# Gate weights of the first block issued from ScalarE, and two output transfers of the last set merged, in a ReGLU MLP

## The chip, the cores and the metric

The kernel runs on one core of a Trainium2 chip. The metric is the device time of one execution, in microseconds (us), as the median of several runs. Engines are named TensorE (PE), VectorE (DVE), ScalarE (ACT), GpSimd (POOL) and SyncE (SP); SP does no arithmetic here and issues most of the transfers. "SPq" in a row of the profile is SP's instruction queue, and a DMA row there is the issue of a transfer, not the transfer.

## The reference

```python
# x: 16 x 256 x 512, w1: 512 x 4096, w2: 2048 x 512, all float32
h = x @ w1
gate, value = np.split(h, 2, axis=-1)
h = np.maximum(gate, 0) * value
return (h @ w2).astype(np.float32)
```

## The kernel before

The 4096 rows of x are taken in four sets of 1024 (`NS` = 4), each of two halves of 512 (`TH`). The hidden size of 2048 is taken in 16 blocks of 128 (`NJ`). Both products are done in fp16 with Strassen's scheme (in Winograd's form): seven products P1 to P7 in place of eight, on sums of x blocks (`x_A..`, `x_S..`) and of weight blocks (`w_B..`, `w_T..`). A `Block` computes one hidden block of the first product with its gate and value; a `Pair` computes 128 rows of each half of the second product. `psx`, `psy` and `psw` are the PSUM banks X, Y and W in the rows of the profile. The first two blocks (`NPLAIN`) of set 0 are computed plainly, class `Plain`, because the sums of x are not ready yet.

PE's and DVE's instructions stay in the order in which they are written, and so do those of ACT, POOL and SP. So every engine runs a list written by hand, and a wait at its head holds all that stands behind it.

The start of the program is what the first part of the change touches. SP issues, in this order: blocks 0 and 1 of x (128 rows, 256 KB each, `fetch_first(0, (0, 1))`, L504); the weights of hidden block 0, first the gate columns and then the value columns (256 KB each, `load_w1`, L224, into the staging tile `w_stage`); blocks 2 and 3 of x; the weights of hidden block 1; four more blocks of x for the second half; and further weights. Blocks 2 and 3 of x, and those of the second half, land in tiles that are used as x tiles or row tiles later (`x_A`, `x_S`, `xh`), and that is how the rows name them: "x_S<-in_x_dram" at 3.23 us is block 3.

PE meanwhile does 28 small and one large matmul on constants (L155, L156) so that it is busy from the start. Then follow, in this order: transposes of x blocks 0 and 1 (L514; copied out of PSUM by DVE and ACT, L517); three filler matmuls (`keep_busy`, L161); the gate part of hidden block 0 for the first 256 columns (L328), which needs the gate weights copied to fp16 by POOL and DVE (`plain_w`, L479); four fillers; the value part; two fillers; the transposes of x block 2 (cast on DVE, L507); three fillers; the transposes of x block 3 (cast on POOL, L507); and the rest of the two plain blocks, with the transposes of the second half between them.

```python
    fetch_first(0, (0, 1))
    first_w = [load_w1(nc.sync, *wl[0])]
    fetch_first(0, (2, 3))
    first_w.append(load_w1(nc.sync, *wl[1]))
```

At the other end, a `Pair` leaves its four pieces of output in a tile `o` of 128 x 2 x 512 and sends them from SP (`send`, L377). Its products end in the order P2, P3 (the two column halves of the first half's rows) and P7, P4 (those of the second half's rows). Where `self.end` holds, each piece of 128 KB is sent as soon as it is written; otherwise the two pieces of one half go together as 256 KB. Before, `self.end` holds for pairs 0, 1 and 3 of the last set. The order of the last set is `LAST_ORDER`; its last product is P4 of pair 3.

Of the kernel before, what the change touches and what calls it, by code (L numbers as in the profile page):

```python
# [26 lines left out]
@with_exitstack  # L27
def kernel(ctx: ExitStack, tc: tile.TileContext, x, w1, w2, out):

    nc = tc.nc
    x2 = x.flatten_outer_dims()
    out2 = out.flatten_outer_dims()
    flagpool = ctx.enter_context(tc.tile_pool(name="flagpool", bufs=1))
    flag = flagpool.tile([1, 1], dt.int32, name="flag")
    with ExitStack() as fast:  # L40
        unfit = fast_way(fast, tc, x2, w1, w2, out2, flag)
    with tc.If(unfit > 0, label="general"):
        with ExitStack() as general:
            general_way(general, tc, x2, w1, w2, out2)
# [52 lines left out]
def fast_way(ctx, tc, x2, w1, w2, out2, flag):  # L97
# [9 lines left out]
    nc = tc.nc  # L107
# [3 lines left out]
    NS = T // (2 * TH)  # L111
    NJ = H // P
    NB = 2 * TH // P
# [107 lines left out]
    def load_w1(eng, jb, n, u, vs=(0, 1)):  # L221
        t = w_stage[:, u:u + n].rearrange("p u v -> p (u v)").rearrange("p (g e j) -> p g e j", g=2, e=4)
        for v in vs:
            eng.dma_start(out=t[:, v], in_=w1_v[v, :, :, jb * P:(jb + n) * P])  # L224
        return t.rearrange("p g (k b) j -> p k b g j", k=2)
# [18 lines left out]
    class Block:  # L244
        def __init__(self, xo, g, jb, in_halves=()):
            self.xo, self.g, self.jb, self.behind, self.in_halves = xo, g, jb, (), in_halves
# [99 lines left out]
    class Pair:  # L346
        def __init__(self, s, g, t):
            self.s, self.t, self.o = s, t, None
            self.end = s == NS - 1 and t != NB // 2 - 2
            o = {f"A{h + 1}{u + 1}": g[:, u * NJ // 2:(u + 1) * NJ // 2, h * TH + t * P:h * TH + (t + 1) * P]  # L350
                 for h in range(2) for u in range(2)}
            o.update({f"S{n + 1}": s_place[:, t % 2, n] for n in range(4)})
            self.op = o
# [93 lines left out]
    wl = [(jb, 1, jb) for jb in range(4)] + [(jb, 2, jb % 6) for jb in range(4, NJ, 2)]  # L447
# [54 lines left out]
    def fetch_first(h, bs):  # L502
        for b in bs:
            nc.sync.dma_start(out=xn[h][b], in_=x_nat[0, h, b])  # L504
# [22 lines left out]
        return psy.tile([P, TH], F32, name="Y", tag="Y")  # L527

    dve, act, pool = nc.vector.tensor_copy, nc.scalar.copy, nc.gpsimd.tensor_copy
    fetch_first(0, (0, 1))  # L530
    first_w = [load_w1(nc.sync, *wl[0])]
    fetch_first(0, (2, 3))
    first_w.append(load_w1(nc.sync, *wl[1]))
    make_identity(nc, ident)
# [284 lines left out]
```

## Time and profile before

| | |
|---|---|
| median of 3 runs | 307.82 us (307.44 to 308.31) |
| profiled execution, its own time | 308.68 us |
| its span, first to last instruction | 306.8 us |
| PE busy | 301.4 us, 98% |
| DVE busy | 237.9 us, 78% |
| ACT busy | 176.6 us, 58% |
| POOL busy | 149.9 us, 49% |
| mean granted TensorE clock | 0.999 |
| moved by DMA | 32.88 MB, mean 107 GB/s |

The profile is of one execution. A line such as "PE X L328 <- POOL w_B L479" means that the instruction of line 328 on PE that writes X waited for POOL's instruction of line 479 that writes `w_B`. The chain that ended last is followed back from the last instruction to what released each step, and in the timeline rows of one form that follow each other are merged, with the start, the length, the engine, the line, the operation and the count.

### The profile page before, as it was taken

The page shows a single profiled execution, that of the slowest core. Times are in us where ns is not written, and L with a number is a line of the kernel's source. Part 1 is how long each engine was busy: PE and PEld are TensorE (multiplying, and loading weights), DVE is VectorE, ACT ScalarE, POOL GpSimd, SP SyncE. Part 2 cuts the span into 40 slices and gives each one's busy share as a digit, 9 for nine tenths or more (in the row PEclk, how much of TensorE's full clock was granted, in tenths as well). Part 3 has the DMA queues.
Part 4 walks back from the last instruction along what each step waited for, and adds up shares of the span by engine and source line. Part 5 has one row for each costly group of instructions (what it writes and reads, how often), then busy time and mean ns, then how long its engine had stood idle before and what let it go on. Part 6 is the DMA issues. An engine that isn't in the chain of part 4 may idle for free.

```text
span 306.8 us, 5361 instructions
## 1 busy us (share of the span) xinstructions
PE 301.4 (98%) x1938; PEld 187.6 (61%) x1938; DVE 237.9 (78%) x393; ACT 176.6 (58%) x351; POOL 149.9 (49%) x187
## 2 busy tenths in 40 slices
PE   7999999999999999999999999999999999999995
PEld 6755554588844444478864444458885444447884
DVE  2599888899778888887627889888545888888861
ACT  2398886445865555537855555545866555553231
POOL 1549999800068999400019989900005899800100
PEclk9999999999999999999999999999999999999999
DMA  7996679955774242000355730000326110000133
GB/s 209 332 297 212 194 172 178 233 113 87 240 208 104 69 77 63 0 2 34 139 170 124 174 81 2 2 0 0 118 89 207 34 35 2 2 0 19 52 105 106
DMA packets 36894, 32.88 MB, mean 107 GB/s; under 512 B 14465, under 2 KB 32385, under 8 KB 36737
## 3 DMA queue, kind: packets, MB, share of 16 engines
q1 hardware_dynamic: 34592, 26.22, 28.5%
q0 software_dynamic: 2272, 6.29, 11.4%
q8 instruction: 16, 0.26, 0.4%
q14 instruction: 14, 0.11, 0.1%
HBM read 27.26 MB, written 12.58 MB: 130 GB/s over the span
## 4 chain that ended last, share of the span: by engine, by line
PE 96%; DMA 2%; SPq 1%; POOL 0%; issue 0%; DVE 0%; ACT 0%
PE Y L252 26%; PE X L252 17%; PE W L252 17%; PE Y L365 14%; PE X L365 9%; PE W L365 9%; DMA x_S<-in_x_dram 2%; PE X L328 1%; PE W L328 1%; PE Y L328 1%; PE Y L514 1%; SPq L504 0%; SPq L224 0%; POOL fold L507 0%; DVE warm L417 0%
## 5 line engine op out<-in xcount | busy, mean ns | idle before, releaser
L252 PEld LDWEIGHTS <-w_T 128*128 128x128 f16 x524 | 51.2, 98 | 54.3 <-POOL w_T L234 0.4
L186 POOL TENSOR_TENSOR fold<-xh 128x1024 f32<-128x1024 f16 x16 | 30.3, 1896 | 95.7 <-DMA xh<-x 68.4
L252 PE MATMUL X<-x_A,w_B 128*128 128x512 f16 x248 | 73.7, 379 | 0.0
L252 PE MATMUL Y<-x_S,w_T 128*128 128x512 f16 x220 | 65.4, 379 | 0.0
L252 PEld LDWEIGHTS <-w_B 128*128 128x128 f16 x372 | 36.3, 98 | 42.2 <-issue 0.2
L280 DVE SCALAR_TENSOR_TENSOR cc<-W,pu 128x512 f32<-128x512 f32 x62 | 42.9, 692 | 19.5 <-ACT pu L274 19.4
L260 ACT COPY Y<-X 128x512 f32<-128x512 f32 x62 | 35.4, 572 | 38.3 <-PE X L252 38.1
L274 ACT ACTIVATE pu<-Y 128x512 f32<-128x512 f32 x62 | 37.1, 598 | 33.8 <-PE Y L252 32.7
L189 POOL TENSOR_TENSOR fold<-fold 128x512 f32<-128x512 f32 (+2 forms) x96 | 51.8, 540 | 7.5
L365 PEld LDWEIGHTS <-w_stage 128*128 128x128 f16 x512 | 50.1, 98 | 5.8
L290 DVE SCALAR_TENSOR_TENSOR cc<-Y,pu 128x512 f32<-128x512 f32 x62 | 42.9, 692 | 6.5
L285 DVE SCALAR_TENSOR_TENSOR g<-X,cc 128x512 f16<-128x512 f32 x62 | 42.9, 691 | 2.3
L302 DVE SCALAR_TENSOR_TENSOR g<-Y,cc 128x512 f16<-128x512 f32 x62 | 42.3, 682 | 1.8 <-PE Y L252 1.8
L365 PEld LDWEIGHTS <-g 128*128 128x128 f16 x384 | 37.6, 98 | 8.2
L267 ACT ACTIVATE pu<-W 128x512 f32<-128x512 f32 x62 | 37.2, 600 | 0.4 <-PE W L252 0.2
L252 PE MATMUL W<-x_S,w_T 128*128 128x512 f16 (+1 forms) x152 | 36.9, 340 | 0.0
L252 PE MATMUL W<-x_S,w_B 128*128 128x512 f16 x124 | 36.9, 379 | 0.0
L252 PE MATMUL Y<-x_A,w_T 128*128 128x512 f16 x124 | 36.9, 379 | 0.0
L365 PE MATMUL X<-w,g 128*128 128x256 f16 x256 | 31.9, 273 | 0.0
L402 DVE SCALAR_TENSOR_TENSOR o<-W,pu 128x256 f32<-128x256 f32 x16 | 6.8, 423 | 21.8 <-PE W L365 21.8
L176 DVE TENSOR_TENSOR w_stage<-g 128x1024 f16<-128x1024 f16 x32 | 21.4, 686 | 0.2
L234 POOL TENSOR_TENSOR w_T<-w_stage,w_T 128x512 f16<-128x512 f32 (+1 forms) x14 | 15.4, 1098 | 5.7 <-DVE w_T L234 5.2
(100 smaller groups left out, 312.0 us busy)
## 6 DMA issues: line engine op xcount, KB each, us to landing
out_dram<-o SPq DMA_DIRECT2D x26, 256.0 KB, 2.0
w_stage<-in_w_dram SPq DMA_DIRECT2D x12, 512.0 KB, 5.3
x<-in_x_dram POOLq DMA_DIRECT2D x4, 1024.0 KB, 10.0
xh<-x SPq DMA_DIRECT2D x16, 256.0 KB, 3.3
w_stage<-in_w_dram SPq DMA_DIRECT2D x8, 256.0 KB, 6.2
w<-in_w_dram POOLq DMA_DIRECT2D x2, 1024.0 KB, 10.4
out_dram<-o SPq DMA_DIRECT2D x12, 128.0 KB, 1.7
x_S<-in_x_dram SPq DMA_DIRECT2D x4, 256.0 KB, 6.0
```

The source lines that it names most:

```text
L176: eng.tensor_tensor(o[n], o[i0], o[i1], op=op)
L186: nc.gpsimd.tensor_tensor(fold, t, t, op=MULT)
L189: nc.gpsimd.tensor_tensor(fold[:, :, :m], fold[:, :, :m], fold[:, :, m:2 * m], op=ADD)
L252: nc.tensor.matmul(ps[:, slice(*c)], wop[wn][:, b, self.jb * P:(self.jb + 1) * P], self.xo[xn][:, b, slice(*c)], start=fresh and b == c[0] ...
L260: nc.scalar.copy(out=self.Y, in_=self.X)
L267: nc.scalar.activation(self.p5, self.W, COPY, scale=GS)
L274: nc.scalar.activation(self.u2, self.Y, COPY, scale=GS)
L280: nc.vector.scalar_tensor_tensor(out=self.c12, in0=self.W, scalar=GS, in1=self.u2, op0=MULT, op1=ADD)
L285: nc.vector.scalar_tensor_tensor(out=self.g[:, self.jb, :TH], in0=self.X, scalar=0.0, in1=self.c12, op0=MAX, op1=MULT)
L290: nc.vector.scalar_tensor_tensor(out=self.c22, in0=self.Y, scalar=GS, in1=self.p5, op0=MULT, op1=ADD)
L302: nc.vector.scalar_tensor_tensor(out=self.g[:, self.jb, TH:], in0=self.Y, scalar=0.0, in1=self.c22, op0=MAX, op1=MULT)
L365: nc.tensor.matmul(ps, self.op[an][:, i], vop[wn][:, i], start=name in ("P1", "P5") and i == 0, stop=i == NJ // 2 - 1, skip_group_check=True)
```

## The change

ScalarE issues the transfer of the gate columns of hidden block 0, written ahead of the first two x transfers, and SP issues only the value columns of that block, in the old place behind the two x transfers. `load_w1` has always had the argument for the engine and for the parts to load. In the last set pair 1 no longer counts as an end pair: its four sends of 128 KB become two of 256 KB. Pair 2 was sent that way before; pairs 0 and 3 are still sent piece by piece.

```diff
@@ class Pair
-            self.end = s == NS - 1 and t != NB // 2 - 2
+            self.end = s == NS - 1 and t in (0, 3)
@@ fast_way
+    first_w = [load_w1(nc.scalar, *wl[0], (0,))]
     fetch_first(0, (0, 1))
-    first_w = [load_w1(nc.sync, *wl[0])]
+    load_w1(nc.sync, *wl[0], (1,))
     fetch_first(0, (2, 3))
     first_w.append(load_w1(nc.sync, *wl[1]))
```

## The prediction

> **What bounds the kernel now.** I read the page first, the waits of PE second, the chain that ended last third, and then the first 14 us piece by piece, because the edit sits at the two ends. The page: TensorE works nearly everywhere, and the DMA engines are fullest at the start.
>
> ```profile
> PE   7999999999999999999999999999999999999995
> DMA  7996679955774242000355730000326110000133
> ```
>
> Each digit is a slice of 7.67 us. Only the first and the last PE digit are below 9, so only time taken out of those two ends can shorten the run. The waits of TensorE's matmuls (us in total, times, longest) name the whole idle time:
>
> ```profile
> PE X L328 <- POOL w_B L479: 1.3, 1, 1.3
> PE Y L418 <- DVE warm L417: 0.9, 1, 0.9
> PE Y L155 <- PEq L803: 0.8, 1, 0.8
> ```
>
> The 1.3 us is the first gate matmul, waiting for the fp16 copy of the weights whose load is moved. It looks like the whole prize. The chain that ended last (start us, us, what) says otherwise:
>
> ```profile
> 2.13 0.51 SPq L224
> ...
> 2.68 0.51 SPq L504
> ...
> 3.23 6.06 DMA x_S<-in_x_dram
> 9.29 0.05 issue
> 9.34 0.63 POOL fold L507
> 9.96 0.05 issue
> 10.01 0.40 PE Y L514 x4
> ```
>
> It runs through block 3 of x (I call it x3): issued at 3.23, landed 9.29, cast on POOL, transposed at 10.01; from there PE is dense. The gate wait at 7.71 is not on it. How near it is comes from the timeline (start us, us, engine line op):
>
> ```profile
> 6.08 0.37 ACT L517 CAST x_A<-X 128x256 f16<-128x256 f32 x1 [0.48 <-PE X L514]
> 7.10 0.29 DVE L479 CAST w_B<-w_stage 128x256 f16<-128x256 f32 x1 [1.02 <-DMA w_stage<-in_w_dram]
> 7.71 0.61 PE L328 MATMUL X<-x_A,w_B 128*128 128x256 f16 x4 [1.33 <-POOL w_B L479]
> 9.47 0.49 PE L161 MATMUL Y<-warm 128*128 128x256 f16 x3
> 10.01 0.40 PE L514 MATMUL Y<-ident,fold 128*128 128x128 f16 x4
> ```
>
> PE is in order. From the gate matmul at 7.71 to the end of the last three filler matmuls (they start at 9.47, and at 0.11 us each, the step of the L161 rows, end at 9.80) it has 2.09 us of its own work, idle parts aside. x3's transposes could start at 9.80 and start at 10.01. So there are **two near-equal limits, 0.21 us apart**: the gate's copy, and x3. An earlier gate alone is worth nothing.
>
> What does x3 wait for? The stretches (us, PE busy, clock, DMA share, GB/s) of TensorE:
>
> ```profile
> 0.00:6.50 6.50, 5.60 (x40) 1.00 0.66 185
> 6.50:7.70 1.20, 0.00 (x0) 1.00 1.01 340
> 7.70:10.00 2.30, 2.25 (x21) 1.00 1.12 346
> 10.00:12.00 2.00, 1.99 (x24) 1.00 1.06 377
> 12.00:14.00 2.00, 2.00 (x23) 1.00 1.18 307
> ```
>
> From 6.5 us on the DMA engines are full (share 1.0 and more), and they are nearly full from 2 us (the one-microsecond stretches give 1.00, 0.94, 0.95, 0.81, 0.87 for 2 to 7). x3 spends 6.06 us in a queue, not in its issue. One more thing from the trace's completion records, sixteen for each transfer, one for each DMA engine: the gate's come at 4.45 to 5.16 us on fifteen engines and at 7.08 on the last. That late engine then also ends value (7.87), x2 (8.56) and x3 (9.29; the other fifteen had it by 8.55).
>
> **The change, part by part.** The sum is made against the profiled execution, 308.68 us (span 306.8 and 1.88 around it). The median of the runs shown is 307.82, so this execution is 0.86 slow; I carry differences over to the median.
>
> SP loses one issue: 0.43 us plus the 0.04 before the next. Value, x2, x3, both parts of block 1's weights and what follows are issued 0.47 us earlier. From the ninth transfer SP is held anyway (x_S issues: median 0.43 us, longest 1.84), so behind that point nothing is gained by a shorter list. SP computes nothing; only loads are queued there.
>
> ScalarE gains one issue, about 0.45 us by SP's rows. Its table load (1.28 us at 0.73) stands beside it; together they end near 2.5, and ScalarE's first copy starts at 5.23. Cost zero, cover 2.7 us. Should the table load come first, the gate is issued at 2.01 instead of 1.66, still ahead of ScalarE's work, and only SP's 0.47 is left. POOL issues no load here; its casts only wait for landings.
>
> The gate's landing: at the soonest 3.3 (0.74 plus the 2.6 that x0 takes alone in an empty queue), at the latest 7.08 as now, if the late engine is as late. I take 5.2, where fifteen engines already had it, since x0, x1 and gate must all pass by then. P1 of the first block then waits for x_A (ready at 6.45 today) and not for weights, and may start 1.0 us earlier (worked out below). PE then idles in front of value or of x2 or x3 instead.
>
> x3's landing is the term that counts. [...] Row first: x3 issued at 3.23, engines full, 6.06 us to land. [...] by the row it is less, since an earlier place in a full queue does not move the bytes ahead of it: x0, x1, gate, value and x2 still have to go first, the same 1.3 MB. What two queues can change is the ramp: between 1.7 and 2.6 us the tenth-microsecond slices average 202 GB/s, against some 390 just after, so 0.9 x (1 - 202/390) = 0.43 us of engine time is lost; two issuers starting together may fill half, 0.2 us. I take -0.2[...], and keep 0 and -0.47.
>
> Behind x3 come the rows of the second half: PE's transposes at 12.18 wait 0.45 for a cast of a block landed at about 11.7, in the same full queue. They move by the same 0.2 or PE waits there; there are only about 0.1 to 0.3 us of slack at each. After 14 us PE's matmuls wait for no input until the last one, and its weight loads only twice, 0.2 us each, for POOL's w_T; so a shift of this size lasts to the end.
>
> The merge: in the last set pair 1 sends twice 256 KB in place of four times 128 KB. SP loses two issues of 0.33 us. The tail (start, us):
>
> ```profile
> 302.44 0.89 PE Y L365 x8
> 303.35 0.39 ACT o L414
> 303.76 0.44 DVE warm L417
> ```
>
> Pair 1's last piece of o is written at 294.13 (ScalarE row at 293.74, 0.39 long), and an output of 256 KB takes 2.0 us to land against 1.7: done near 296.5, 7 us before the last piece. Its buffer is not needed again: pair 3 takes the slots of the first two pu2 tiles. So zero. The cover is those 7 us; uncovered it would cost 0.3. ScalarE's queue is a third one in use; no row prices its setting up, and I take zero, bounded by a few tenths either way inside the 1.88 around the span.
>
> Sum: -0.2 (x3 and its followers) + 0 (ScalarE) + 0 (merge) = 308.5 for the profiled execution, 307.6 for the median.
>
> **Rivals.** *The gate was what held the late engine.* If its 2 us of delay belongs to the position of that load, and vanishes, x3 lands with the fifteen others or sooner (at least 0.74 earlier) and the limit becomes x_A. x1 shares the engines with 256 KB more, about 0.87 us at 300 GB/s: it lands at 4.94 instead of 4.07; from the start of its transposes to the ready x_A are 1.67 us (4.78 to 6.45); P1 at about 6.7, 1.0 us earlier. Time 306.8. For it: fifteen engines are early. Against: nothing says why the one is late, and x2, x3 and the second half must all follow.
>
> *x1 falls behind the gate (slower).* [...] No row of before shows two such queues at once here; by the rows' one queue x1 lands at 4.07[...]. If the late engine is late again, x1 lands with it, at 7.08: x_A at 7.08 + 0.05 + 1.67 = 8.80, P1 at 8.85, x3's transposes at 8.85 + 2.09 = 10.94 in place of 10.01, that is +0.93, 308.75. It decides once x1 lands after 6.15 (10.01 - 2.09 - 0.1 - 1.67). For it: x1 has the longer way to PE than the gate, and the gate is put ahead of it. Against: it needs a stall of 2 us on one engine in just that load.
>
> *The change does nothing at all*: table load first, the same full queue: 307.8.
>
> **Numbers.** Chances: forecast 0.54, late engine gone 0.25, x1 late 0.13, nothing 0.08. A measurement of this kernel can tell about 0.3%, 0.92 us, from no change. The forecast and the last case lie within it. The gain of 1.0 is just beyond it, and a larger ramp gain or a saving in what lies around the span may add to it: faster 0.26. x1 late by the full amount is just beyond on the other side: slower 0.12. Same 0.62. Range 306.7 to 308.6: the -1.0 case to most of the +0.93 case; the likeliest case's own is 307.3 to 308.0.
>
> **What the changed profile would show.** The gate's cast on DVE directly behind the copies of x_A, and no 1.3 us of PE X L328 waiting for POOL w_B; a wait of the same size in front of value, x2 or x3; x3's cast on POOL at 9.1 instead of 9.34. ScalarE's issue at 0.74, the table load behind it. x1's transposes at 4.78 or a few tenths later. Tail unchanged from 303 us less the shift. I am wrong if x3's cast starts before 8.7 (gain near 1 us), or if L514's X transposes start after 6.2 (loss), or if the time outside the span moves.

## The result, and the profile after

The changed kernel takes 307.03 us (median of 6 runs, 306.84 to 307.43) against 307.95 us before (6 runs). The ratio is 0.9972, 95% interval 0.9959 to 0.9984: about 0.9 us shorter, within the stated range and just inside the 0.3% that was called no change. The forecast step was -0.2 us; the measured one is closer to the -1.0 of the first rival. The profiled execution takes 307.43 us, with a span of 305.6.

In what follows x0 to x3 are the first four blocks of x, and gate and value are the two weight loads of hidden block 0; SP or ScalarE issues each of them. The page's slices, to set beside those of before:

```profile
PE   8999999999999999999999999999999999999996
DMA  7996679955774260000355820000326110000133
```

Only the two end digits of PE rise. The waits of TensorE's matmuls (us in total, times, longest):

```profile
PE Y L418 <- DVE warm L417: 0.9, 1, 0.9
PE Y L155 <- PEq L804: 0.8, 1, 0.8
PE X L514 <- DMA x_A<-in_x_dram: 0.6, 1, 0.6
PE Y L514 <- POOL fold L507: 0.2, 1, 0.2
```

The 1.3 us behind the gate's copy is gone. In its place are a wait for x1 (0.6 us) and one for x3 (0.2 us). The beginning in order of time (start us, us, engine line op):

```profile
0.74 0.44 ACTq L224 DMA_DIRECT2D w_stage<-in_w_dram  x1
1.21 1.28 ACT L517 ACT_TABLE_LOAD   x1 [1.21 <-PEq L804]
4.75 0.39 POOL L479 CAST w_B<-w_stage 128x256 f16<-128x256 f32 x1 [3.45 <-DMA w_stage<-in_w_dram]
5.45 0.66 PE L514 MATMUL X<-ident,x_A 128*128 128x128 f32 x4 [0.64 <-DMA x_A<-in_x_dram]
6.41 0.83 PE L328 MATMUL X<-x_A,w_B 128*128 128x256 f16 x4
9.19 0.40 PE L514 MATMUL Y<-ident,fold 128*128 128x128 f16 x4 [0.23 <-POOL fold L507]
```

ScalarE issues at 0.74 with the table load behind it, at no cost: the load ends at 2.49, and ScalarE's first copy starts at 4.85. The gate has landed by 4.70; x1 comes only at 5.41 (4.07 before), and TensorE waits 0.64 us for it, with the three fillers on constants held behind. The first gate matmul starts 1.3 us earlier than before. The chain that ended last (start us, us, what) still leads to x3:

```profile
2.13 0.51 SPq L504
...
2.68 5.79 DMA x_S<-in_x_dram
8.46 0.05 issue
8.52 0.63 POOL fold L507
9.14 0.05 issue
9.19 0.40 PE Y L514 x4
```

x3 lands at 8.46 where it landed at 9.29, and its transposes start at 9.19 where they started at 10.01. From there everything moves as one piece: from the start of these transposes to the last copy of o on ScalarE are 293.34 us before and 293.38 after. The stretches of the start (us, PE busy, clock, DMA share, GB/s):

```profile
0.00:6.50 6.50, 5.08 (x41) 1.00 0.72 210
6.50:7.70 1.20, 1.14 (x10) 1.00 1.08 346
7.70:10.00 2.30, 2.07 (x27) 1.00 1.12 345
10.00:12.00 2.00, 2.00 (x19) 1.00 1.08 368
```

TensorE now works from 6.5 to 7.7; the DMA engines moved 210 GB/s up to 6.5 us in place of 185. The difference lies between 4 and 7 us. First before, where PE is followed by the other engines, then after; the last two numbers are again DMA share and GB/s:

```profile
4.00:5.00 1.00, 1.00 (x6) 0.86 (x5) 0.19 (x1) 0.00 (x0) 0.00 (x0) 1.00 0.95 256
5.00:6.00 1.00, 1.00 (x7) 0.92 (x7) 0.57 (x2) 0.37 (x1) 0.00 (x0) 1.00 0.81 201
6.00:7.00 1.00, 0.38 (x4) 0.09 (x1) 0.09 (x1) 0.37 (x1) 0.00 (x0) 1.00 0.87 259
```

```profile
4.00:5.00 1.00, 0.81 (x5) 1.00 0.96 317
5.00:6.00 1.00, 0.55 (x5) 1.00 0.96 301
6.00:7.00 1.00, 0.94 (x9) 1.00 1.00 355
```

The engines are a little busier and move about a third more. The end is not only shifted (start us, us, what):

```profile
301.66 0.89 PE Y L365 x8
...
302.57 0.39 ACT o L414
...
302.99 0.44 DVE warm L417
```

This copy of o starts 0.78 us earlier, but the span is 1.14 us shorter. The other 0.36 us lies behind the last landing, at 305.44 before and 304.68 after. SP closes the program with waits on counters (semaphores); the trace lists sixteen raises of a counter for each send, for the last one at 305.30 to 305.44 us before and at 304.54 to 304.68 after. The instructions of that line on SP, first from 305.44 us on in the kernel before, then from 304.68 on in the kernel after:

```profile
L814 SPq EVENT_SEMAPHORE  x7: 28/28/28, 305.5 to 305.8; - x7
```

```profile
L815 SPq EVENT_SEMAPHORE  x1: 28/28/28, 304.7 to 304.7; - x1
```

Seven waits of 0.06 us each (start to start) stand against one. That accounts for 6 x 0.06 = 0.36 us.

### The profile page after: what moved, and what is told of

Same layout as the page of the kernel before. It is cut to its first block, busy times and chain, and to the rows that moved or that the text cites. A ratio compares the mean times of both kernels' runs of the same rounds, so it can differ in the third digit from the quotient of the medians.

```text
span 305.6 us, 5356 instructions
## 1 busy us (share of the span) xinstructions
PE 301.0 (98%) x1938; PEld 186.8 (61%) x1938; DVE 238.0 (78%) x393; ACT 176.5 (58%) x351; POOL 149.6 (49%) x187
## 4 chain that ended last, share of the span: by engine, by line
PE 96%; DMA 2%; SPq 1%; POOL 0%; issue 0%; DVE 0%; ACT 0%
PE Y L252 26%; PE X L252 18%; PE W L252 18%; PE Y L365 14%; PE X L365 9%; PE W L365 9%; DMA x_S<-in_x_dram 2%; PE X L328 1%; PE W L328 1%; PE Y L328 1%; PE Y L514 1%; SPq L504 0%; POOL fold L507 0%; DVE warm L417 0%; SPq L224 0%
```

## The experiments

**The kernel before, once more.**

> The kernel before, unchanged, to see whether the late DMA engine belongs to it or to one execution. If the gate load behind x0 and x1 on one queue is what makes an engine late, the gate's copies on POOL and DVE again start near 7.1 us and block 3's cast on POOL near 9.3; ratio 1.000. If lateness is a matter of chance, the cast of block 3 starts anywhere from 8.4 to 9.4, and the ratio is still 1.000.

Measured: 1.0003 (0.9994 to 1.0011); x3 landed at 8.56, not at 9.29, and no DMA engine was 2 us late with the gate (5.26). So the very late DMA engine on which I built two rivals belongs to single executions. The kernel still took 308.06 us in the median: the time before is not explained by that engine.

**Each part alone.** Only the start of the diff:

```diff
+    first_w = [load_w1(nc.scalar, *wl[0], (0,))]
     fetch_first(0, (0, 1))
-    first_w = [load_w1(nc.sync, *wl[0])]
+    load_w1(nc.sync, *wl[0], (1,))
```

> Only the gate load moved to ScalarE, the sends left in four pieces. My theory: all of the gain is here: ratio 0.997, block 3's cast near 8.5 us, a wait of about 0.6 us for x1. Rival (the merge brings a part, or the end does): a ratio of 0.999 or more and the rest in the merge alone.

Measured: 0.9975 (0.9964 to 0.9986). x3 landed at 7.55. And only the merge:

```diff
-            self.end = s == NS - 1 and t != NB // 2 - 2
+            self.end = s == NS - 1 and t in (0, 3)
```

> Only the two sends merged. My theory: 1.000 within 0.001, chain of the end unchanged, since these pieces land 7 us before the last. Rival: two issues of 0.33 us less on SP show as 0.3 to 0.6 us, ratio 0.998 to 0.999.

Measured: 0.9983 (0.9974 to 0.9991), 0.5 us less. My theory that the merge costs and brings nothing fell. The profile shows why: one closing wait stands behind the last landing, as in the changed kernel. In the trace of before the sends take eight counters in turn, numbers 102 to 109, and SP's closing waits go over them in this order. With fourteen sends after the last row load, the last send falls on the second counter of that round, 103. Its wait stands at 305.46 us, and those on the other six, whose sends had landed by 303.71, still stand behind it, at 305.52 to 305.82. With two sends fewer it falls on the last of the eight (109 in the changed kernel, its wait at 304.70).

**The same number of sends, with pair 1 merged and pair 2 in pieces.** It asks whether merging pair 1 is worth something by itself, with the number of sends and the place of the last one in the round as before.

```diff
-            self.end = s == NS - 1 and t != NB // 2 - 2
+            self.end = s == NS - 1 and t in (0, 2, 3)
```

> The start of before; pair 1 of the last set sends merged as in the change, but pair 2 sends in pieces, so SP issues as many sends as before. My new theory, the drain: SP's closing waits go over the completion counters in a fixed order, transfers take the counters in turn, and what counts is how many waits stand behind the counter of the last send (seven in before, one with the merge alone, 0.06 us each). Then this kernel has seven again, ratio 1.000. Rival: larger and fewer sends of pair 1 are worth 0.4 us by themselves, ratio 0.9985.

Measured: 1.0003 (0.9996 to 1.0009). From 304.80 us on, where its last send landed, SP's closing line reads:

```profile
L814 SPq EVENT_SEMAPHORE  x7: 28/28/28, 304.8 to 305.2; - x7
```

Pair 1 is merged as in the change, and nothing is gained. This run can't part fewer sends as such from the place of the last one, since both are as before. The place rests on the tails: from the last landing to the end of the span are 1.32 to 1.34 us in all ten profiles with fourteen sends, and 0.96 in all four with twelve. Of the 0.5 us (0.3 to 0.8) measured for the merge alone the waits explain 0.36; whether there is more is not shown.

**Do the parts add?** The changed kernel and the gate-only kernel were run again, with more runs.

> The changed kernel beside the others on one chip. If the two parts add up (0.9975 and 0.9983), ratio 0.9958; if the first comparison was right, 0.997 and a part of one is lost in the other. Block 3's cast on POOL between 7.6 and 8.5 us; one wait of the drain behind the last landing.

> The gate-only kernel again, to see whether the two parts add. If they add: 0.9985 or so here (0.36 us over the whole change at 0.9973), seven waits behind the last landing. If the merge is lost behind the moved gate, 0.9973 and as long a tail as with the change.

Measured: 0.9974 (0.9965 to 0.9984) for the change, 0.9981 (0.9974 to 0.9988; 16 runs) for the gate alone, whose profile has seven waits behind the last landing. With the first value of the gate alone the product of the parts, 0.9958, lay outside the interval of the change. With the longer measurement it is 0.9981 x 0.9983 = 0.9964, whose difference to 0.9974 is inside the intervals. So the parts may well add: about 0.6 us from the gate and 0.36 us, the count of closing waits, from the merge. In the second run of the change the chain no longer goes through x3 (start us, us, what):

```profile
1.20 4.18 DMA x_A<-in_x_dram
...
5.43 0.66 PE X L514 x4
6.09 0.33 PE Y L161 x3
6.42 0.57 PE X L328 x4
6.99 0.44 PE Y L161 x4
7.42 0.44 PE W L328 x4
7.86 0.22 PE Y L161 x2
8.08 0.22 PE Y L514 x4
8.30 0.33 PE Y L161 x3
```

It comes from x1 over the gate matmuls and TensorE's own list, fillers included, to x3's transposes at 8.68. Both gate-only profiles have the same chain (8.55 and 8.72).

**The order without the second queue.** First the gate ahead of both x blocks, all on SP:

```diff
+    first_w = [load_w1(nc.sync, *wl[0], (0,))]
     fetch_first(0, (0, 1))
-    first_w = [load_w1(nc.sync, *wl[0])]
+    load_w1(nc.sync, *wl[0], (1,))
```

> The gate goes ahead of x0 and x1, but on SP's own queue, value in its old place: the order changes, the queue does not. If the order (gate ahead of the x blocks) brings the gain: gate landed by about 3.5 us, x1 by 5.0, block 3's cast near 8.5, ratio 0.997 or a little less. If a second queue is needed: block 3 lands near 9.3 as before, since SP's list is as long as before, and the ratio is 1.000; then nothing is won by order. If x1 is held back by more than 1 us: over 1.000.

Measured: 1.0054 (1.0038 to 1.007), slower by 1.7 us. x1 landed at 6.23, only 0.8 us later than with the change, and x3 at 8.93. What is different stands in the lengths of the rows (start us, us, engine line op):

```profile
6.27 1.12 PE L514 MATMUL X<-ident,x_A 128*128 128x128 f32 x4 [0.84 <-DMA x_A<-in_x_dram]
7.18 0.85 PE L161 MATMUL Y<-warm 128*128 128x256 f16 x3
7.82 1.06 PE L328 MATMUL X<-x_A,w_B 128*128 128x256 f16 x4
```

The same four transposes take 0.66 us after the change, the same fillers 0.49 in the second run of it: here TensorE still runs at about half speed. The trace's clock record puts full speed at 9.71 us here; in the other profiles it is between 3.76 and 6.79. My reading was that the rise of the clock was put off while TensorE waited for x1. The profile is one of five runs of 309.65 to 309.89 us. Three others took 308.1 to 308.7, and four took 310.2 to 310.4 with a mean granted clock of 0.994 in place of 0.998; the profile does not speak for those. To test the reading, six fillers go, on top of the gate's move, between the transposes of x0 and those of x1:

```diff
     turn_first(xo, 0, 0, halves(*YS), (dve, act))
+    keep_busy(6)
     XS = [new_x(), new_x()]
     turn_first(xo, 0, 1, halves(*XS), (dve, act))
```

> The gate ahead of x0 and x1 on SP (1.0054 before), now with six filler matmuls between the transposes of x0 and those of x1, where TensorE was idle. If the loss came from the idle time, which put off the rise of the clock (full speed from 9.7 us in that profile), the clock is up by 7 us and the ratio falls to 0.998 to 1.000. If the loss came from x1's late landing itself, it stays at 1.005.

Measured: 1.0013 (1.0003 to 1.0024). The profiled run, of 309.25 us, is one of the longest of its 22. In it one DMA engine was 2.1 us late with x1, which landed at 7.59, later than ever, and yet:

```profile
7.63 0.66 PE L514 MATMUL X<-ident,x_A 128*128 128x128 f32 x4 [1.30 <-DMA x_A<-in_x_dram]
8.13 0.49 PE L161 MATMUL Y<-warm 128*128 128x256 f16 x3
```

That is full speed (from 5.7 us), and no run of the 22 has a granted clock below 0.998. The fillers win back 0.4% of the 0.54%: most of the loss was the clock. The remaining 0.13% may be x1's lateness; this profile shows that it costs, but not that it makes up the median. Second, the gate between x0 and x1:

```diff
-    fetch_first(0, (0, 1))
-    first_w = [load_w1(nc.sync, *wl[0])]
+    fetch_first(0, (0,))
+    first_w = [load_w1(nc.sync, *wl[0], (0,))]
+    fetch_first(0, (1,))
+    load_w1(nc.sync, *wl[0], (1,))
```

> All on SP, in the order x0, gate, x1, value: the loads mix as they do with two queues, and SP's list is as long as before. If what counts is that gate and value no longer follow each other in one queue, block 3's cast starts at 8.0 or earlier and the ratio is about 0.9975. If the second queue (or the shorter list of SP) is needed, 1.000. If x1 comes so late that PE idles before its clock has risen, as in the run with the gate first, over 1.002, with the x1 transposes at half speed.

Measured: 1.0071 (1.0047 to 1.0095). Its seven runs fall in two groups, 307.68 and 307.87 us, and 310.09 to 311.10. The profile is of the first group: full speed from 3.9 us, x1 landed at 6.01, x3 at 8.22, and the clock stayed up over a wait of 1.42 us for x1. There is no profile of the second group, but each run's granted clock is on record: 0.993 or 0.994 in four of its five runs, 1.000 and 0.999 in the first group. In the one profile here with 0.993 (the kernel before without fillers, below) the clock rose early and then fell to half for 3.41 us, so a fall, and not a late rise, is the likelier reading for those four. The fifth has 0.998, as the profile with the gate first.

**Another load on ScalarE's queue.** x1 in place of the gate:

```diff
-    fetch_first(0, (0, 1))
+    nc.scalar.dma_start(out=xn[0][1], in_=x_nat[0, 0, 1])
+    fetch_first(0, (0,))
     first_w = [load_w1(nc.sync, *wl[0])]
```

> x1 instead of the gate is issued on ScalarE; sends as before. SP's list is shorter by one as in the gate-only kernel, x1 is not behind the gate, and gate and value follow each other again on SP. If the shorter list or the second queue is the cause, ratio 0.9975 or a little less, and no wait for x1 at its transposes. If moving the gate away from value is the cause, 1.000 and block 3's cast at 8.5 to 9.3.

Measured: 0.9983 (0.9975 to 0.9991), the same as the gate alone in its longer measurement. x1 landed at 4.17 and x0 at 4.38, before the gate (5.10), and x3 at 8.45. That profile is of a run of 307.99 us, the second longest of thirteen, and its x3 comes about as late as in the repeat of before (8.56); so the gain is shown by the times, not by the profile. So it does not matter much which of the first three loads leaves SP's list; that gate and value follow each other again on SP does not undo the gain.

**Without the fillers.** The nine behind the first gate matmuls are left out, once after and once before the change:

```diff
     plain[0].part("gate", *first_half, cols(0, 2))
-    keep_busy(4)
     plain[0].part("value", *first_half, cols(0, 2))
...
-    keep_busy(2)
     turn_first(xo, 0, 2, [t[:, 2] for t in turned], (dve, act))
-    keep_busy(3)
     turn_first(xo, 0, 3, [t[:, 3] for t in turned], (dve, act))
```

> The changed kernel without the nine filler matmuls that stand behind the first gate matmuls (four, two and three). In the gate-only run and the second run of the change the chain goes through x1, the gate matmuls and these fillers, 0.99 us of them. If TensorE's own list is the new limit, block 3's transposes start as soon as its cast is done, 0.1 to 0.4 us earlier: ratio 0.996 to 0.997. Rival: block 3's landing still limits, ratio 0.9973 as with fillers. Third: the idle time takes the clock down, over 1.000 with transposes at half speed.

> The kernel before without the same nine fillers. In before the fillers lie in the shadow of block 3's landing, so nothing is gained: 1.000, block 3's cast where it was (8.6 to 9.3). Rival: TensorE's list limits here too, 0.998. Third: clock down, over 1.002.

Measured after the change: 0.9966 (0.9953 to 0.9979), the shortest median of all, 306.91 us, but its interval overlaps that of the change, so a gain is not shown. x3 landed at 7.91 and its transposes started at 8.63, with TensorE waiting 0.5 us for the cast: with the fillers gone x3 limits again at once. Measured before the change: 1.0004 (0.9988 to 1.0019), as expected, but three of its fourteen runs took 309.8 us or more, each with a granted clock of 0.993; of the 46 runs of the kernel before beside them none took more than 309.07. The profiled one is such a run; its stretches (us, PE busy, clock, DMA share, GB/s):

```profile
9.00:10.00 1.00, 0.94 (x8) 1.00 1.08 342
10.00:11.00 1.00, 0.55 (x8) 0.86 0.81 298
11.00:12.00 1.00, 1.00 (x12) 0.50 0.97 331
```

The clock fell to half at 10.7 us and stayed there for 3.41 us. TensorE had waited 2.7 us for the gate's copy (one DMA engine late, landed 7.49), 0.3 for value's copy and 0.5 for x3, without fillers between. In the kernel before they cost nothing that the medians show, and the runs without them include three long ones. After the change five runs were too few to see that.

## Why the prediction was right or wrong

The forecast of no clear change held by luck: 0.28% was measured, just under the 0.3% that the prediction took as the border, and its sum was -0.2 us against -0.9. The two limits were right, and two terms were too small: x3's landing and the merge.

*Two near-equal limits, everything behind x3's transposes rigid*: right. With a load on ScalarE the chain goes now through x3 and now through x1 and the gate matmuls. That an earlier gate alone is worth nothing was not shown by itself, since moving it always moved other loads too. From the start of x3's transposes to the last copy of o are 293.2 to 293.4 us in every profile but the one whose clock fell.

*x3's landing moves by 0.2 us*: this term was too small. In the profiles with the old order on SP (before, its repeat, merge alone, pair 2 in pieces) x3's transposes start at 10.01, 9.29, 9.18 and 9.33; with the gate on ScalarE (the change twice, gate alone twice) at 9.19, 8.68, 8.55 and 8.72. The medians are 9.31 and 8.70: 0.6 us. My argument was that the bytes ahead of x3 stay the same and that the engines are full. The bytes do stay the same, but I took a busy share for a speed. Between 4 and 7 us the engines of before were busy 0.81 to 0.95 of the time and moved 239 GB/s; from 7 to 10 us they moved 350. Over all profiles the rate from 4 to 7 us is 239 to 305 GB/s in the eight with all first loads on SP, and 324 to 351 in the six with one on ScalarE. The trace has sixteen completion records for each transfer, one for each DMA engine, and x3's cast waits for the last: it is at 9.29 before, and the cast starts at 9.34. The completions of x3 (trace, us):

| kernel | first engine | mean of 16 | last engine |
|---|---|---|---|
| before, repeat, merge alone, pair 2 in pieces | 7.03, 6.75, 6.66, 6.94 | 8.00, 7.69, 7.65, 7.51 | 9.29, 8.56, 8.46, 8.61 |
| the change twice, gate alone twice | 7.09, 6.98, 7.05, 7.13 | 7.57, 7.33, 7.29, 7.45 | 8.46, 7.95, 7.55, 7.86 |

The filled ramp, from which I took the 0.2, did not occur: from 2 to 3 us the engines moved 208 GB/s against 299 before, and the gate's packets begin in earnest only at 2.8 us, 2.1 after their issue. What changes lies behind 4 us: the engines move more, and the last ones fall less far behind the first. Why they do so when a load leaves SP's list is not settled: a shorter list and a second queue always came together here, and a kernel that has one without the other was not run.

*SP's list shorter by one issue, kept at -0.47 as one end*: by the rows it is 0.55, since x3 was issued at 2.68 in place of 3.23. The gate alone measures 1 - 0.9981 = 0.19%, 0.58 us, with an interval of 0.37 to 0.80. Both figures are inside it, and closer than my 0.2. It fits too that nothing is gained with the gate first or second on SP, where x3 is issued at 3.28 and 3.23. Against it stands that x3's first engine is done no earlier than before, so the earlier issue did not simply arrive at x3. No run parts the shorter list from an effect of the second queue.

*The merge is zero, covered by 7 us*: wrong, by the 0.36 us of six closing waits. The cover of the transfer was right, and beside the point: I followed the data of pair 1 to its landing and did not count what SP does after the last landing. The seven closing waits are in the trace of before.

*P1 about 1.0 us earlier, x1 at 4.94*: the first gate matmul, which the prediction calls P1, came 1.3 us earlier in the profile; x1 was later than estimated, 5.41. That x1 shares with the gate was an estimate that no row of before could show; here both queues move at once. The packets of the changed kernel, first from 2.8 to 3.2 us, then from 3.2 to 4.8 (packets, MB, share; q1 is SP's queue, q10 ScalarE's):

```profile
q1 hardware_dynamic: 33, 0.05, 56.3%
q10 hardware_dynamic: 98, 0.05, 41.3%
```

```profile
q1 hardware_dynamic: 255, 0.34, 59.3%
q10 hardware_dynamic: 430, 0.21, 44.5%
```

So x0 and x1 share with the gate, but not evenly: equal bytes in the first 0.4 us, then, from 3.2 to 3.6, 0.03 MB of x against 0.11 of the gate, and more of SP's later.

*Rival: the late engine gone, -1.0*: the size is near, and its sign in the profile (x3's cast before 8.7) appeared. Its mechanism is not confirmed: the one engine that is 2 us late shows in three of eight profiles with all loads on SP (before, the gate first with fillers, before without fillers) and in none of six with two queues, too few to tell from chance; and the repeat of before was no faster without it. One half of the rival came true: in the second run of the change and in both of the gate alone the limit is x1's block with the gate matmuls behind it.

*Rival: x1 behind the gate, slower*: it did not happen in the change, where x1 (5.41) stays below the point of 6.15. With the gate first on SP x1 comes at 6.23 and the kernel is slower, but mainly by something that I had left out, the clock (full speed only at 9.71 us; with the fillers, from 5.7 us, the loss is 0.13% in place of 0.54%). The prediction moved TensorE's idle time about at its own length. That held in before, where the clock was up from 5.91 us and stayed up over 1.33 us of waiting; it failed where 0.84 us came before the rise, and where 2.7 us and two shorter waits came after it (half speed for 3.41 us).

*ScalarE and the third queue at zero*: right. About 1.9 us lie around the span in the profile before and 1.8 after, but the runs of both kernels spread alike, from 1.7 to 1.9.

## What to carry to other kernels

x3 could be cast only when the slowest of the DMA engines had done its share, here at 9.29 us before, with the first at 7.03: read the bytes moved and not the busy share, and compare the first and the last completion, before calling a full queue a fixed sum of bytes. At the start of a program, put ahead what has the longest way to TensorE (with the gate ahead of x1 in SP's list the kernel was 0.54% and 0.71% slower), and keep TensorE busy until its clock is up (six fillers in the wait for x1 brought the 0.54% down to 0.13%); here 0.84 us of waiting before the rise, which came at 9.71 us, did more harm than 1.33 us after it. At the end, count what the closing engine still does after the last landing: here the number of sends set where in a round of eight waits the last one fell, and two sends fewer moved the end by 0.36 us.

## What the runs showed of the hardware that was not expected

The gate's transfer, issued by ScalarE at 0.74 us, had its first packet at 2.81 us, while SP's first one, issued at the same time, moved from 1.77. That is not ScalarE's queue as such: in the run with x1 on ScalarE, x1, issued there at 0.73, moved from 1.75, and then SP's x0, issued at 0.74, began only at 2.32. No run settles what makes one of the two begin later.

TensorE's clock reached full speed anywhere between 3.76 and 6.79 us in thirteen profiles that share the list of warm-up matmuls, and at 9.71 us in the one where TensorE had waited 0.84 us for x1 from 5.43 on. The fall at 10.7 us (the kernel before without fillers) lasted 3.41 us, and 6.83 us lie between the rise before it and the fall. It came with no idle piece longer than 2.7 us.

The last send of 128 KB landed either about 2.1 or about 2.3 us after its copy on ScalarE started, without a pattern by kernel.
